# A decoder step on one core: another recorded order of the attention's blocks

## The chip, the cores and the metric

The kernel runs on one core of a Trainium2 chip. A core has TensorE (PE) for matmuls, VectorE (DVE), ScalarE (ACT) and GpSimd (POOL) for elementwise work, and SyncE (SP), which here only issues DMAs. Each engine takes its instructions in the order in which they were emitted. The metric is the device time of one execution in microseconds (us). The kernel before took 1256.64 us, the median of three runs (1256.27 to 1256.86).

## The reference, cut to what matters

One inference step of a two-layer trunk with D = 1024, for a prompt of 512 tokens and for 8 samples of 8 new tokens each. Layer 0 is a recurrent block with a SwiGLU; then keys and values are made once; layer 1 is attention over a sliding window of 128 with a learned sink per head, and a SwiGLU. The change lies in the attention:

```python
q = apply_partial_rope((h @ attn_w_q[j]).reshape(B, T, N_HEADS, HEAD_DIM), pos)
out = sliding_sink_attention(q, k_all, v_all, attn_sinks[j], p0) @ attn_w_o[j]
x = x + g1[:, None, :] * out

def sliding_sink_attention(q, k_all, v_all, sinks, p0):
    ...
    s = jnp.einsum('bnqkgd,bnskd->bnkgqs', qg, kb).astype(jnp.float32) * (HEAD_DIM ** -0.5)
    ...
    m = jnp.maximum(jnp.max(s, axis=-1, keepdims=True), sink)
    e = jnp.exp(s - m)
    p = e / (jnp.sum(e, axis=-1, keepdims=True) + jnp.exp(sink - m))
    o = jnp.einsum('bnkgqs,bnskd->bnqkgd', p.astype(vb.dtype), vb)
    return o.reshape(B, T, N_HEADS * HEAD_DIM)
```

A prompt block of 128 queries sees its own 128 keys and the 128 before them; the 8 tokens of a sample see the 128 cached keys of that sample and the new ones.

## The kernel before, in words

Activations lie transposed, features on the 128 partitions, tokens along the free dimension. The tokens are split into two halves, A and B (h = 0 and 1 in the code), each with 256 prompt tokens and 4 samples of 8 tokens: 288 columns. Weights are fp32 and are cut, after loading, into a high part and the rest (`convert`, line 1034: a cast on ScalarE and a subtraction on VectorE), and so are the activations; one product of a 128-column block of a 1024-row weight with one half is 8 x 3 = 24 matmuls of 128x288 (`product`, line 1070). The converted weights lie in ten slots named `wh`, two for each weight block; two of the ten hold the keys during attention. `load_more` (line 1025) issues the weight loads on SP's queue.

The attention stage is a list of blocks, written down by hand in the string `ATT` (line 53). A name is a letter, a number and the half:

- `q0` to `q7`: one of the eight blocks of the query projection, a product of 24 matmuls. Its evacuation (`rope`, line 1547) is a shuffle, a multiplication and an addition on VectorE and one multiplication and two small copies on GpSimd. `q7` also opens the half's operand buffer `h` for the output projection (`attn_open`, line 1805): the chunks that are finished by then are cut into two parts there.
- `a0` to `a7`: attention of the prompt for two heads of that query block (`attn_chunk`, line 1650). Scores (matmuls over 64 rows, `mm<-wh,sl` in the profile), maxima with the mask on VectorE (`CUSTOM_DVE_ANT_0`), exponentials on ScalarE, sums and reciprocals on VectorE, scaling on three engines. A second part follows later: transposes, copies, the value product (`ada<-td,sl`) and its cut into two parts.
- `s0` to `s3`: attention of one sample for all heads (`attn_sample`, line 1730): two DMAs for the cached keys and values, transposes of the keys, scores (`mm<-ta,reg`, `mm<-tb,reg`), softmax; a second part with transposes and value products (`mm<-td,reg`, `mm<-td,wh`). The cached keys and values of samples 0, 3 and 6 share one buffer, those of 1, 4 and 7 another, those of 2 and 5 a third (line 1737); s0B to s3B are samples 4 to 7.
- `f`: closes a half (`attn_fin`, line 1829): writes the new keys out and puts the samples' results into the operand buffer `h`, which every output product of that half reads.
- `o0` to `o2`: the first output products of a half (24 matmuls each). The rest of them, and the half B of these, follow in the next stage.

The second part of a block is not recorded at once. It waits in a list (`flush`, line 1638) until one or two more blocks have been recorded; `f` records all that wait. All `a` and `s` blocks take their small statistics (maximum, sum, reciprocal) from two tiles in turn (`new_stat`, line 1646).

The string does not set the order on the engines directly. Every operation is first recorded with its reads and writes; its place in the record is its priority. Then a planner (`schedule`, line 227) with costs written into the code goes through the record and emits, on each engine, the operation that can start first. Ties and near ties go by the record: the key is the possible start plus 0.75 ns for each place (lines 39 and 344). On TensorE an operation of another shape (scores over 64 rows, products with 64 columns) counts as 100 ns later than one of the same shape (line 339). It looks up to 600 places ahead of the oldest operation that is left (lines 50 and 316), and SP's DMAs stay within 60 places of their order. PSUM has six tiles for products, scores and transposes (line 43) and two for value products. What an engine runs on the chip is the planner's order.

Of the kernel before, what the change touches and what calls it, by code (L numbers as in the profile page):

```python
# [49 lines left out]
WIN = 600  # L50

RNN = "x0 x1 x2 g0 g1 x3 y0 y1 x4 g2 g3 x5 y2 x6 y3 g4 g5 x7 y4 y5 g6 g7 y7 y6"
ATT = "q0A q2A a0A q1A q0B a2A q1B q3A a0B q2B q4A a1A a1B a4A a3A q3B a2B q5A q4B a3B q6A a5A q5B q7A a6A a4B s0A q6B a5B s1A s2A s3A q7B a7A s0B fA s2B a6B a7B s1B o0A s3B o1A o2A fB"
LOOK = {"PE": 24, "DVE": 24, "ACT": 24, "POOL": 24, "SP": 24}
NRAW = 4
FILL = 250
# [459 lines left out]
def trunk_kernel(ctx, tc, a):  # L516
# [1339 lines left out]
    each = []  # L1856
    for w in ATT.split():
        h, n = "AB".index(w[-1]), int(w[1:-1] or 0)
# [245 lines left out]
```

## Time and profile before

| | |
|---|---|
| timed runs | 1256.27, 1256.64, 1256.86 us |
| profiled execution | 1259.39 us |
| its span, first to last instruction | 1257.6 us |
| TensorE busy | 1243.6 us (99%) |
| VectorE, ScalarE, GpSimd busy | 897.9, 659.4, 481.4 us |
| mean granted TensorE clock | 0.995 |
| attention stage, about | 700 to 809 us of the span |

The page of the profile gives each engine's busy time, the chain of work that ended last, and groups of instructions by the names of their tiles. All instructions stand under line 489, the line of the helper that records them, so they are told apart by tile names, shapes and times. A windows view gives, for stretches of time, the busy time of each engine with the number of its instructions, the granted clock of TensorE as a share of full speed, the share of DMA time and GB/s. A timeline row gives start, length, engine, operation and tiles, and the number of equal instructions that were merged.

### The profile page before, as it was taken

The numbers are of one execution on the slowest core, as the hardware profiler recorded it, in microseconds if no ns is written. First come the engines' busy times: TensorE is split into PE (matmuls) and PEld (weight loads), VectorE is DVE, ScalarE is ACT, GpSimd is POOL, SyncE is SP. The second block draws the span as 40 slices with busy tenths as digits, with TensorE's granted clock in tenths as the row PEclk, the third lists the DMA queues.
The fourth block names the chain that finished last, engine by engine and source line by source line (L and its number), as shares of the span: only waits on it lengthen the run. The fifth ranks groups of instructions, "written<-read, shape, count | busy, mean of one in ns | idle before, by whom it ended". The sixth has DMA issues, their size and how long they took to land.

```text
span 1257.6 us, 25624 instructions
## 1 busy us (share of the span) xinstructions
PE 1243.6 (99%) x9674; PEld 1181.1 (94%) x9674; DVE 897.9 (71%) x2192; ACT 659.4 (52%) x1474; POOL 481.4 (38%) x671
## 2 busy tenths in 40 slices
PE   8999999999999999999999999999999999999997
PEld 7888999999998999999999987999999999999997
DVE  6989784776674676467579878558767658756856
ACT  4798963753342354145357678538425425524533
POOL 3478550133451453345125446100435336435510
PEclk9999999999999999999999999999999999999999
DMA  9966454417455645445423322232333323323222
GB/s 313 300 203 222 155 166 154 156 56 214 152 178 179 202 128 181 156 153 184 116 77 73 78 60 60 77 99 97 91 95 85 101 84 100 96 76 100 79 91 76
DMA packets 221838, 165.42 MB, mean 132 GB/s; under 512 B 23725, under 2 KB 206985, under 8 KB 221682
## 3 DMA queue, kind: packets, MB, share of 16 engines
q1 hardware_dynamic: 221266, 163.45, 42.4%
q8 instruction: 76, 1.25, 0.4%
q14 instruction: 48, 0.39, 0.1%
q0 software_dynamic: 448, 0.32, 0.1%
HBM read 160.85 MB, written 4.87 MB: 132 GB/s over the span
## 4 chain that ended last, share of the span: by engine, by line
PE 90%; DVE 4%; ACT 4%; issue 1%; DMA 0%; POOL 0%; DVEq 0%; ACTq 0%; SPq 0%; POOLq 0%
PE mm L489 86%; PE ada L489 5%; ACT ta L489 1%; DVE sl L489 1%; ACT sl L489 1%; DVE wh L489 1%; DVE ta L489 1%; ACT tb L489 0%; DVE tb L489 0%; ACT wh L489 0%; ACT L489 0%; DMA raw<-in_ffn_w_out_dram 0%; DVE h L489 0%; ACT td L489 0%; ACT h L489 0%
## 5 line engine op out<-in xcount | busy, mean ns | idle before, releaser
L489 PE MATMUL mm<-h,wh 128*128 128x288 f32 x4128 | 590.5, 297 | 1.1 <-DVE wh L489 0.9
L489 PEld LDWEIGHTS mm<-h,wh 128*128 128x128 f32 x4128 | 559.3, 188 | 12.9 <-issue 6.0
L489 PE MATMUL mm<-sl,wh 128*128 128x288 f32 x3218 | 461.1, 296 | 0.6 <-DVE wh L489 0.5
L489 PEld LDWEIGHTS mm<-sl,wh 128*128 128x128 f32 x3218 | 436.7, 188 | 7.5 <-issue 5.9
L489 ACT CAST wh<-raw 128x512 fp32r<-128x512 f32 (+3 forms) x388 | 268.8, 711 | 300.6 <-PE mm L489 188.4
L489 DVE TENSOR_TENSOR wh<-raw,wh 128x512 fp32r<-128x512 f32 (+3 forms) x388 | 352.7, 929 | 50.0 <-ACT wh L489 45.0
L489 POOL TENSOR_TENSOR raw<-raw 128x512 f32<-128x512 f32 x76 | 112.2, 1476 | 191.4 <-DVE wh L489 135.0
L489 DVE SCALAR_TENSOR_TENSOR x<-mm,mods,x 128x256 f32<-128x256 f32 x160 | 77.2, 483 | 125.9 <-PE mm L489 125.4
L489 POOL TENSOR_TENSOR x<-x,ta 128x32 f32<-128x32 f32 x120 | 42.4, 353 | 243.9 <-DVE ta L489 243.8
L489 POOL TENSOR_TENSOR raw<-raw,raw 128x512 f32<-128x512 f32 x76 | 113.0, 1486 | 4.2
L489 PE MATMUL mm<-tb,wh 128*128 128x288 f32 (+1 forms) x488 | 89.0, 297 | 1.6 <-DVE td L489 1.6
L489 POOL TENSOR_TENSOR td<-td,td 128x288 f32<-128x288 f32 x38 | 31.1, 820 | 131.3 <-ACT td L489 131.3
L489 PEld LDWEIGHTS mm<-tb,wh 128*128 128x128 f32 x488 | 72.8, 188 | 3.0 <-DVE td L489 2.0
L489 ACT ACTIVATE ta<-x 128x288 f32<-128x288 f32 (+1 forms) x56 | 24.3, 442 | 62.5 <-POOL x L489 44.0
L489 PE MATMUL mm<-ta,wh 128*128 128x288 f32 (+1 forms) x254 | 56.0, 297 | 0.0
L489 DVE TENSOR_TENSOR td<-mm,td 128x288 f32<-128x288 f32 x76 | 33.6, 452 | 25.4 <-PE mm L489 25.1
L489 PE MATMUL ada<-reg,cz 128*32 128x512 f32 (+1 forms) x408 | 47.2, 547 | 0.0
L489 PEld LDWEIGHTS mm<-ta,wh 128*128 128x128 f32 x254 | 41.7, 188 | 1.7 <-ACT sl L489 0.8
L489 ACT COPY td<-mm 128x256 f32<-128x256 f32 (+1 forms) x102 | 33.6, 354 | 13.9 <-PE mm L489 13.6
L489 DVE TENSOR_TENSOR sl<-td,sl 128x288 fp32r<-128x288 f32 x50 | 33.7, 674 | 6.0 <-ACT sl L489 5.7
L489 ACT ACTIVATE ta<-ta,stat 128x256 f32<-128x256 f32 (+2 forms) x72 | 32.5, 474 | 9.4 <-DVE stat L489 9.1
L489 DVE TENSOR_TENSOR mm<-mm,ta 128x288 f32<-128x288 f32 x38 | 17.7, 465 | 27.5 <-PE mm L489 27.5
(213 smaller groups left out, 1305.3 us busy)
## 6 DMA issues: line engine op xcount, KB each, us to landing
raw<-in_ffn_w_in_dram SPq DMA_DIRECT2D x88, 512.0 KB
reg<-in_ada_w_dram SPq DMA_DIRECT2D x72, 512.0 KB
raw<-in_ffn_w_out_dram SPq DMA_DIRECT2D x32, 384.0 KB
raw<-in_ffn_w_out_dram SPq DMA_DIRECT2D x32, 320.0 KB
raw<-in_rnn_w_in_dram SPq DMA_DIRECT2D x16, 512.0 KB
reg<-in_kv_ada_w_dram SPq DMA_DIRECT2D x14, 512.0 KB
wh<-in_ada_w_dram SPq DMA_DIRECT2D x24, 256.0 KB
raw<-in_rnn_w_out_dram SPq DMA_DIRECT2D x8, 512.0 KB
```

The costliest lines, as they stand in the source:

```text
L489: self.rec.add(eng, lambda: getattr(obj, name)(*map(real, args), **{k: real(v) for k, v in kw.items()}), cost, outs, ins, func, lat, port, ...
```

## The change

One string is replaced. In words, for what moves:

- front: q0B and q1A are recorded ahead of q2A and a0A; a4A ahead of a1A and a1B; q3B ahead of a3A;
- the end of half A: q6B is recorded behind s3A, next to q7B, where it stood between s0A and a5B;
- behind a7A: s0B, s1B, a6B, fA, a7B, o0A, s2B, s3B where there was s0B, fA, s2B, a6B, a7B, s1B, o0A, s3B.

The stretch from q5A to s0A is the same. The set of blocks, and so of operations, is the same.

```diff
-ATT = "q0A q2A a0A q1A q0B a2A q1B q3A a0B q2B q4A a1A a1B a4A a3A q3B a2B q5A q4B a3B q6A a5A q5B q7A a6A a4B s0A q6B a5B s1A s2A s3A q7B a7A s0B fA s2B a6B a7B s1B o0A s3B o1A o2A fB"
+ATT = "q0A q0B q1A q2A a0A a2A q1B q3A a0B q2B q4A a4A a1A a1B q3B a3A a2B q5A q4B a3B q6A a5A q5B q7A a6A a4B s0A a5B s1A s2A s3A q6B q7B a7A s0B s1B a6B fA a7B o0A s2B s3B o1A o2A fB"
```

## The prediction, made before the change was run

> **What bounds the kernel now.** I read the page first, then the chain, then the windows of the attention stage (it runs from about 700 to 809 us), and last the rows of single engines inside it.
>
> ```profile
> span 1257.6 us, 25624 instructions
> ...
> PE 1243.6 (99%) x9674; PEld 1181.1 (94%) x9674; DVE 897.9 (71%) x2192; ACT 659.4 (52%) x1474; POOL 481.4 (38%) x671
> ...
> PE 90%; DVE 4%; ACT 4%; issue 1%; DMA 0%; POOL 0%; DVEq 0%; ACTq 0%; SPq 0%; POOLq 0%
> ```
>
> TensorE has work for 1243.6 of 1257.6 us and the chain that ends last lies on it for 90%. To find the rest I cut the attention stage into pieces of 10 us (columns: TensorE, its weight loads, VectorE, ScalarE, GpSimd busy; granted clock; DMA):
>
> ```profile
> 720.00:730.00 10.00, 10.00 (x93) 8.71 (x92) 8.49 (x43) 9.87 (x36) 3.06 (x6) 1.00 0.18 52
> 730.00:740.00 10.00, 10.00 (x95) 8.75 (x93) 8.22 (x34) 7.18 (x26) 4.34 (x10) 1.00 0.01 4
> 740.00:750.00 10.00, 10.00 (x86) 9.61 (x83) 8.73 (x41) 7.46 (x26) 3.74 (x7) 1.00 0.45 133
> ...
> 760.00:770.00 10.00, 10.00 (x91) 9.33 (x91) 9.22 (x38) 9.70 (x39) 4.76 (x13) 1.00 0.05 15
> 770.00:780.00 10.00, 9.54 (x94) 7.53 (x90) 8.78 (x38) 8.32 (x31) 8.76 (x17) 1.00 0.20 57
> 780.00:790.00 10.00, 9.87 (x60) 6.89 (x58) 6.25 (x36) 5.95 (x24) 1.98 (x9) 0.66 0.55 161
> 790.00:800.00 10.00, 10.00 (x89) 9.83 (x89) 4.59 (x21) 5.44 (x19) 2.07 (x5) 1.00 0.22 65
> ```
>
> Read the PE column and PEclk. TensorE is full until 770 and again from 790. Between, it has 0.59 us without work, and from 780 to 790 the granted clock is 0.66: 10 x (1 - 0.66) = 3.4 us of clock are lost. VectorE and ScalarE are nearly full from 760 to 770 (9.22 and 9.70). They, not TensorE, set the speed of the softmax there. The next view is the same stage for the weight products alone, matmuls that read the activations `h` (columns: busy time with their number, clock, DMA):
>
> ```profile
> 752.50:759.00 6.50, 0.11 (x1) 1.00 0.01 3
> 759.00:770.00 11.00, 7.58 (x48) 1.00 0.05 13
> 770.00:780.80 10.80, 0.00 (x0) 1.00 0.23 66
> 780.80:787.70 6.90, 0.00 (x0) 0.51 0.67 196
> 787.70:809.00 21.30, 14.84 (x90) 1.00 0.17 49
> ```
>
> The products of the query projection are used up before 770. From 770 to 787.7 there is not one of them. These 17.7 us hold only sample blocks, transposes and the last chunks, small matmuls whose inputs come from the softmax of the block before, and here the clock falls to 0.51 for 6.9 us. After 787.7 the output products run packed and TensorE stays full but for the last few microseconds of the kernel (350.23 of the last 357.60, below), so every microsecond by which they begin earlier or later goes into the end one for one. That start waits for two things: the value product of chunk a7A and the closing step fA of the first half.
>
> ```profile
> 900.00:1257.60 357.60, 350.23 (x2653) 349.15 (x2651) 243.59 (x504) 149.67 (x290) 132.00 (x135) 0.99 0.31 92
> ```
>
> I named the blocks by laying the recorded order beside the rows:
>
> ```profile
> 764.27 0.38 PE L489 MATMUL mm<-ident,wh 128*128 128x128 f32 x2
> ...
> 765.29 0.30 PE L489 MATMUL mm<-ta,reg 128*64 128x160 f32 x1
> ...
> 766.13 3.31 PE L489 MATMUL mm<-h,wh 128*128 128x288 f32 x23
> ...
> 770.65 0.30 PE L489 MATMUL mm<-ta,reg 128*64 128x160 f32 x1
> ...
> 787.75 0.65 PE L489 MATMUL mm<-h,wh 128*128 128x288 f32 x3
> ```
>
> The 23 matmuls at 766.13 are q7B, the last product. At 764.27 stand two transposes of sample block s2A, in the first cluster after q6B; at 765.29 the scores of s0A and s1A; at 770.65 the scores of s2A and s3A, only after q7B and a value product; at 787.75 the first output product, o0A.
>
> **The change part by part.** No instruction is added or dropped. Each engine gets the same set; priorities, the order of the two shared statistics tiles, and the positions in the queues change.
>
> *Statistics tiles.* Attention blocks use two tiles in turn, so a block's maxima wait for the block two places before it. Up to a7A the turn of the second stretch (a5A to a7A) stays the same, block by block. At the tail s1B takes the place of s2B and the reverse; the two are alike in size. In the front a4A takes the place of a1A, and a1A and a1B fall back by one.
>
> *q6B moved behind s3A* (24 matmuls; on VectorE a shuffle, a product and a sum; on GpSimd one product and two copies; no DMA). The first half's sample blocks now rank ahead of it. Its evacuation shares VectorE with the maxima of a5B, and behind these the chain is:
>
> ```profile
> 767.63 1.23 DVE L489 TENSOR_TENSOR wh<-raw,wh 128x1024 fp32r<-128x1024 f32 x1
> 768.77 0.41 DVE L489 TENSOR_TENSOR stat<-stat 128x4 f32<-128x4 f32 x1
> ...
> 771.50 0.31 DVE L489 CUSTOM_DVE_ANT_0 ta<-mm,reg 128x160 f32<-128x160 f32 x1
> ...
> 775.74 0.27 DVE L489 CUSTOM_DVE_ANT_0 ta<-mm,reg 128x128 f32<-128x128 f32 x1
> ```
>
> At 767.63 the low-part conversion of output weight 2 (1.23 us) runs ahead of the sum of a5B at 768.77, which holds the tile that s2A needs. That tile is free at 768.77 + 0.41 = 769.18, but s2A's maximum starts at 771.50, since its scores are issued at 770.65. That is 2.3 us on the chain a5B, s2A, a7A (775.74), a7A's value product, o0A. In the new order the transposes of s1A and s2A rank ahead of q6B's 24 matmuls, so s2A can be ready when the scores of s0A and s1A go at 765.29, and 769.18 becomes the bound. I take -2.3 us. The conversion needs the slots that q6 leaves (keys, q6, q7 and outputs 0 and 1 hold the ten), so it moves behind a later q6B. That is worth at most 768.77 - 767.63 = 1.1 us; as a5B's exponentials still end inside this time I take half, -0.5 us. Bounds of both: -3.4 if all of it counts; 0 if the planner fills the same gaps with q6B as now; above, +3.3 us, the length of one product (the row at 766.13), if one more product stands between s2A's transposes and its scores. What hides q6B itself today is the wait of the softmax chain from 759 to 770, where 7.58 us of products lie; if that cover is gone, q6B moves into the hole at 770 and fills it, which costs nothing.
>
> *q7B, a7A, s0B* keep their places; s3A, q6B and q7B now follow one another. q7B also carries six copies on ScalarE and six subtractions on GpSimd that open the second half; they stay ahead of a7A, as now: 0.
>
> *The tail.* s1B (two DMAs, four matmul steps, three ScalarE, four GpSimd and three VectorE steps, and behind them four matmul steps and two VectorE steps for its values) moves ahead of a6B; s2B moves behind o0A. What decides is the DMA queue, which issues in order:
>
> ```profile
> 759.45 0.33 SPq L489 DMA_DIRECT2D reg<-in_cache_k_dram  x1
> 771.98 0.33 SPq L489 DMA_DIRECT2D reg<-in_cache_v_dram  x1
> ```
>
> The second cache load of s3A held SP's queue from 759.45 to 771.98. s1B's key load goes to the tile that s2A leaves, behind that same wait; its value load needs s2A finished. s2B has an own tile that comes free with s3A. The scores of either wait for a statistics tile behind a7A anyway: 0, within 0.7 us either way (two loads of 0.33 us that change places). fA (two transposes, three ScalarE steps, one VectorE step, eight small output DMAs) is recorded behind s1B and a6B, and a6B's value steps ahead of it. Its inputs come from s3A, so it still becomes ready with it; its DMAs fall behind two more cache loads and nobody on the chip waits for them: 0. o0A is recorded one block earlier, and its four weight loads with it; they fill tiles needed after 800: 0.
>
> *The front.* q0B, q1A ahead of q2A and a0A: 48 matmuls of the same length in another order with TensorE full, and a0A's scores wait for nothing but a statistics tile: 0. a4A ahead of a1A, a1B, and q3B ahead of a3A:
>
> ```profile
> 714.44 0.28 DVE L489 CUSTOM_DVE_ANT_0 ta<-mm,reg 128x128 f32<-128x128 f32 x1
> ...
> 717.77 0.45 DVE L489 TENSOR_TENSOR sl<-mm,ta 128x288 f32<-128x288 f32 x1
> ```
>
> At 714.44 a1A's maxima begin. In the new order that turn belongs to a4A, whose queries are finished only at 717.77 + 0.45 = 718.2. So the softmax falls back by 3.8 us here. TensorE has q3B as cover (3.3 us of product) and stays full. The lag has to be made up before the products run out: from 730 to 740 ScalarE is busy 7.18 of 10 and VectorE 8.22 of 10, from 740 to 750 7.46 and 8.73. Together 5.4 us of ScalarE and 3.0 us of VectorE are free, against at most 3.8 us that slipped. I take 0, with +3.8 us as the upper end and 0 as the lower.
>
> *Changes of shape on TensorE.* Each switch between products and the 64-row or 64-column batches costs about a quarter of a microsecond (1.5 us in 6 cases, in the row below, for the value products from 745 to 810), and the new order makes a few more or fewer: 0, within 0.5 us either way.
>
> ```profile
> PEld ada L489 <- issue: 1.5, 6, 0.7
> ```
>
> **Sum.** -2.3 - 0.5 + 0 = -2.8 us. The profiled execution took 1259.39 us (span 1257.6, 1.8 around it), 2.75 us above the median of the timed runs, 1256.64. On the profiled one it gives 1256.6, on the median 1253.8 us. The clock loss is left in place: the stretch without products only gets shorter, from 17.7 to about 15 us.
>
> **The rivals.**
>
> *The clock keeps full speed (faster still).* The clock fell at 780.8 with TensorE busy 9.54 of 10 in the slice before. So it was not idle time as the rows count it, and the stretch without products is the one thing that sets the place apart. If a part of q6B or q7B falls into 770 to 787, the 6.9 x 0.49 = 3.4 us come back: 1253.8 - 3.4 = 1250.4. Against it: the planner issues whatever is ready first, and products always are. The Trainium skill ("TensorE: Matmul & The Clock Gate", part 1) says that the half clock comes after at least one idle window of about 3.4 us; by that rule alone no order of this kind matters, and nothing would be won here. This trace disagrees, as the rows above show no such idle time. Part 4 of the same page says that transposes do not count as busy in the same way, which would fit the stretch.
>
> *The planner undoes it (no change).* It takes on each engine the instruction that can start first and weighs the recorded position with 0.75 ns a place. q6B falls back by some 110 places, 80 ns. Today it runs in gaps of the softmax; if it runs in the same gaps, all of the second stretch stays as it is: 1256.6.
>
> *The lag of the front is not made up (slower).* If a7A's maxima, at 775.74 today, come the whole 3.8 us later, the start of o0A does too: 1256.6 + 3.8 = 1260.4. It decides against the forecast once more than 2.8 + 2.5 us of delay is left at a7A, or more than 2.5 us if the gain fails. For it: ScalarE had 9.87 of 10 from 720 to 730 and 9.70 from 760 to 770, so what slips there is not made up there. Against it: the free 5.4 and 3.0 us between.
>
> *The scores crowd out the products (slower).* Sample scores that are ready early hold a PSUM tile until their statistics tile is free, and there are six such tiles. If q7B has to wait for one, it ends behind the chain: + 3.3 us, 1259.9. It decides if TensorE shows more than 2.5 us without work between 755 and 770, where it has none now.
>
> **How the numbers follow.** A measurement of this kernel tells about 0.2% (2.5 us) from no change. Forecast 0.31, with an own range from 1252.7 (the whole -3.4 and -0.5 for shapes) to 1255.4 (half of the 2.3 us); clock kept 0.08; no change 0.29; lag 0.20; crowding 0.12. Faster takes the first two, less the 0.03 of the forecast that would end within 0.2%: 0.36. Within 0.2% is 0.29 + 0.03 = 0.32, slower 0.20 + 0.12 = 0.32. The lower end reaches a little into the case of the clock, 1250.8, and the upper end to the whole lag, 1260.6.
>
> **What would show it.** Right: s2A's maximum begins within half a microsecond of the end of a5B's sum, a7A's maxima come 2 to 3 us earlier against the start of the stage, and the first output product follows the last query product by about 15 us. The lag: a4A's maxima begin only after q4A's queries, and the blocks up to a5A run later than before. The clock: no slice under 0.9 near 780. Wrong altogether: q6B in the same gaps, or a hole for TensorE before 770.

## The result, and the profile after

| | before | after |
|---|---|---|
| median of 15 timed runs each, us | 1256.86 | 1259.91 |
| ratio, 95% interval | | 1.002 (1.0013 to 1.0027) |
| profiled execution, us | 1259.39 | 1259.54 |
| its span, us | 1257.6 | 1257.8 |
| mean granted clock | 0.995 | 0.998 |

The change costs about 3 us, 0.2%. The forecast was 1253.8 us, 2.8 us faster. The two profiled executions look alike only because that of before has a stretch of half clock: a second trace of the same kernel (experiment 4) took 1256.63 us and has none. Of the 15 timed runs of before four lie between 1258.5 and 1259.1 us, and of 102 more, taken beside the experiments, 22 lie above 1258 us at a lower mean clock (0.994 to 0.997). The same stretch of time, the windows view of the first trace of before and then of the second (columns as in the prediction):

```profile
780.84:787.66 6.82, 6.69 (x36) 4.06 (x33) 3.77 (x23) 3.06 (x13) 1.23 (x4) 0.50 0.67 196
```

```profile
780.84:787.66 6.82, 6.39 (x56) 5.20 (x56) 6.01 (x39) 5.27 (x23) 0.93 (x3) 1.00 0.67 198
```

Clock 0.50 in the one, 1.00 in the other, with one and the same order. From here on, "before" is the second trace. The page of after:

```profile
span 1257.8 us, 25623 instructions
...
PE 1242.1 (99%) x9674; PEld 1180.4 (94%) x9674; DVE 897.1 (71%) x2192; ACT 658.6 (52%) x1474; POOL 480.7 (38%) x671
...
PE 89%; DVE 5%; ACT 4%; issue 1%; DMA 1%; POOL 0%; DVEq 0%; ACTq 0%; SPq 0%; POOLq 0%
```

TensorE is still busy for 99%; in the chain of waits a DMA now has 1% where it had 0%. The attention stage by windows, before and then after:

```profile
700.00:710.00 10.00, 10.00 (x81) 9.61 (x81) 9.30 (x42) 7.39 (x24) 4.84 (x10) 1.00 0.36 90
710.00:720.00 10.00, 10.00 (x94) 8.28 (x93) 8.60 (x48) 7.60 (x30) 4.38 (x13) 1.00 0.19 54
760.00:770.00 10.00, 10.00 (x96) 9.41 (x97) 9.22 (x38) 9.70 (x38) 5.32 (x14) 1.00 0.04 13
770.00:780.00 10.00, 9.54 (x87) 7.29 (x83) 8.51 (x39) 8.13 (x30) 8.77 (x20) 1.00 0.22 63
780.00:790.00 10.00, 9.57 (x81) 7.88 (x80) 7.81 (x46) 8.05 (x33) 2.36 (x8) 1.00 0.66 192
```

```profile
700.00:710.00 10.00, 9.01 (x71) 8.23 (x70) 7.33 (x38) 4.25 (x16) 3.65 (x7) 1.00 0.19 53
710.00:720.00 10.00, 9.89 (x91) 8.60 (x93) 7.85 (x36) 7.95 (x28) 4.88 (x13) 1.00 0.19 54
...
760.00:770.00 10.00, 9.65 (x90) 8.40 (x88) 8.05 (x41) 9.31 (x39) 2.76 (x10) 1.00 0.05 14
770.00:780.00 10.00, 9.88 (x99) 8.33 (x95) 9.14 (x40) 8.02 (x26) 7.73 (x18) 1.00 0.19 54
780.00:790.00 10.00, 9.96 (x79) 7.78 (x79) 8.94 (x49) 9.04 (x39) 5.39 (x13) 1.00 0.26 70
```

TensorE loses 0.99 us at 700 to 710, in the front, where the prediction had nothing; from 770 to 790 it has less idle time than before (0.16 us against 0.89), and from 760 to 770 more (0.35 us against none).

To place the loss I compare the start of the same instruction in both traces: the first shuffle of q0A on VectorE, which opens the stage, and a weight conversion behind its last block. Before, then after:

```profile
687.42 0.49 DVE L489 STREAM_SHUFFLE ta<-mm 128x288 f32<-128x288 f32 x1
814.69 1.23 DVE L489 TENSOR_TENSOR wh<-raw,wh 128x1024 fp32r<-128x1024 f32 x1 [0.36 <-ACT wh L489]
```

```profile
687.92 0.50 DVE L489 STREAM_SHUFFLE ta<-mm 128x288 f32<-128x288 f32 x1
816.65 1.23 DVE L489 TENSOR_TENSOR wh<-raw,wh 128x1024 fp32r<-128x1024 f32 x1 [0.37 <-ACT wh L489]
```

The stage takes 127.27 us before and 128.73 after: 1.46 us are lost inside it. The 0.50 us at its opening arise before any instruction has changed its place: over all the traces this opening lies between 686.70 and 688.51 and has nothing to do with the order. Behind the stage more is lost, at one weight load of the feed-forward stage. Its second weight comes in loads of 320 KB, and ScalarE casts each when it has landed. The casts of loads 2 to 5 (columns: start, length, engine, operation, tiles, shapes; in brackets the idle time ahead and who ended it), before, then after:

```profile
900.92 0.73 ACT L489 CAST wh<-raw 128x640 fp32r<-128x640 f32 x1 [2.21 <-DMA raw<-in_ffn_w_out_dram]
904.62 0.73 ACT L489 CAST wh<-raw 128x640 fp32r<-128x640 f32 x1 [0.90 <-DMA raw<-in_ffn_w_out_dram]
906.06 0.73 ACT L489 CAST wh<-raw 128x640 fp32r<-128x640 f32 x1
909.39 0.73 ACT L489 CAST wh<-raw 128x640 fp32r<-128x640 f32 x1 [2.60 <-PE mm L489]
```

```profile
902.57 0.73 ACT L489 CAST wh<-raw 128x640 fp32r<-128x640 f32 x1 [1.96 <-DMA raw<-in_ffn_w_out_dram]
907.09 0.72 ACT L489 CAST wh<-raw 128x640 fp32r<-128x640 f32 x1 [1.49 <-DMA raw<-in_ffn_w_out_dram]
908.34 0.73 ACT L489 CAST wh<-raw 128x640 fp32r<-128x640 f32 x1
911.86 0.73 ACT L489 CAST wh<-raw 128x640 fp32r<-128x640 f32 x1 [2.79 <-PE mm L489]
```

From cast 2 to cast 3 pass 3.70 us before and 4.52 after, from cast 2 to cast 5 8.47 and 9.29. TensorE itself waits there for 0.48 us, which it does not before:

```profile
908.50 1.71 PE L489 MATMUL mm<-h,wh 128*128 128x288 f32 x11 [0.48 <-ACT td L489]
```

So the lateness against before is 0.50 us at 687, 1.96 at 816, 2.47 at 911 and 2.9 at the end (span 1254.9 against 1257.8).

### The profile page after: what moved, and what is told of

The parts are those of the page before. It is cut to its first block, busy times and chain, and to the rows that moved or that the text cites. A ratio compares the mean times of both kernels' runs of the same rounds, so it can differ in the third digit from the quotient of the medians.

```text
span 1257.8 us, 25623 instructions
## 1 busy us (share of the span) xinstructions
PE 1242.1 (99%) x9674; PEld 1180.4 (94%) x9674; DVE 897.1 (71%) x2192; ACT 658.6 (52%) x1474; POOL 480.7 (38%) x671
## 4 chain that ended last, share of the span: by engine, by line
PE 89%; DVE 5%; ACT 4%; issue 1%; DMA 1%; POOL 0%; DVEq 0%; ACTq 0%; SPq 0%; POOLq 0%
PE mm L489 84%; PE ada L489 5%; ACT ta L489 1%; DVE ta L489 1%; DVE sl L489 1%; DMA raw<-in_ffn_w_out_dram 1%; ACT sl L489 1%; ACT tb L489 1%; DVE tb L489 1%; DVE wh L489 1%; ACT L489 1%; ACT td L489 0%; ACT wh L489 0%; DVE td L489 0%; DVE h L489 0%
```

## The experiments

The theories:

- 1: the new front makes the softmax late and TensorE waits (1a: because of q0B and q1A; 1b: because of a4A).
- 2: q6B and q7B together push a7A back.
- 3: the weight load is late by chance.
- 4: TensorE's own work, and not the softmax, fills the stretch before a7A.
- 5: the order makes the load late.
- 6: a fetch of instructions makes it late.

The table has all runs, with the number of the experiment. The stage is the time between the two rows above (shuffle of q0A and weight conversion); a row without a ratio is a single execution; the last two columns are the casts' distances.

| run | median us | before, beside it | ratio (95%) | stage us | cast 2 to 3 | cast 2 to 5 |
|---|---|---|---|---|---|---|
| before, again (4) | 1256.63 | 1257.11 | | 127.27 | 3.70 | 8.47 |
| changed kernel | 1259.91 | 1256.86 | 1.002 (1.0013 to 1.0027) | 128.73 | 4.52 | 9.29 |
| front alone (1) | 1259.29 | 1257.11 | 1.0011 (1.0002 to 1.0021) | 128.83 | 3.48 | 8.39 |
| middle alone (2) | 1257.66 | 1257.11 | 1.0005 (0.9996 to 1.0013) | 127.22 | 4.32 | 9.10 |
| tail alone (3) | 1257.48 | 1257.11 | 1.0002 (0.9993 to 1.0011) | 127.36 | 3.42 | 8.33 |
| q0B, q1A early (5) | 1258.79 | 1256.81 | 1.0007 (0.9996 to 1.0017) | 128.55 | 3.60 | 8.52 |
| a4A early (6) | 1257.14 | 1256.81 | 1.0004 (0.9995 to 1.0012) | 127.04 | 3.47 | 8.39 |
| middle and tail (7) | 1258.27 | 1256.81 | 1.0008 (1.0 to 1.0017) | 127.20 | 4.60 | 9.37 |
| before, q6B short (8) | 1259.03 | 1256.81 | 1.0019 (1.001 to 1.0028) | 129.41 | 3.48 | 8.38 |
| changed, again (9) | 1259.89 | 1256.75 | 1.0024 (1.0015 to 1.0033) | 128.76 | 4.47 | 9.24 |
| middle, again (10) | 1257.16 | 1256.75 | | 127.20 | 4.38 | 9.15 |
| front and tail (11) | 1259.18 | 1256.75 | 1.0016 (1.0007 to 1.0025) | 128.91 | 3.93 | 8.71 |
| changed, fetch moved (12) | 1258.92 | 1256.98 | 1.0011 (1.0002 to 1.002) | 128.74 | 3.59 | 8.50 |
| before, fetch moved (13) | 1256.8 | 1256.98 | 0.9999 (0.999 to 1.0008) | 127.17 | 3.48 | 8.39 |

A ratio is estimated from all the runs and is not the quotient of the two medians: for q0B and q1A early the medians differ by 1.98 us, the ratio says 0.9 us, and its interval contains no change at all. The intervals are about 1 us wide to either side. Parts of 1 us are therefore judged by the traces, where the stage repeats to 0.1 us for one and the same order at full clock (127.27 and 127.17; 128.73, 128.76 and 128.74; 127.22 and 127.20).

**1. The front alone.** Only the front of the new string:

```diff
-q0A q2A a0A q1A q0B a2A q1B q3A a0B q2B q4A a1A a1B a4A a3A q3B a2B
+q0A q0B q1A q2A a0A a2A q1B q3A a0B q2B q4A a4A a1A a1B q3B a3A a2B
```

> Only the front of the order is the new one (q0B and q1A early, a4A ahead of a1A and a1B, q3B ahead of a3A); the rest is as before. Theory 1, the lag of the front stays: in the trace of the changed kernel the blocks from a2B to a6A stand 1.5 us later than before, although TensorE is full. If that is the cause, this run alone is 1.2 to 1.8 us slower than before (1258 to 1258.5 us against 1256.6) and shows the same 1.5 us from 743 us on. Theory 2, the two products in a row behind s3A: no effect here, within 0.5 us of before. Theory 3, the late weight load at 907 us: this run shows it or not whatever its front is.

The stage takes 128.83 us, 1.56 more than before, as theory 1 says; the load at 907 us is not late (cast 2 to 3: 3.48). The front carries the whole loss of the stage.

**2. The middle alone.**

```diff
-s0A q6B a5B s1A s2A s3A q7B a7A s0B
+s0A a5B s1A s2A s3A q6B q7B a7A s0B
```

> Only q6B is moved behind s3A, next to q7B; front and tail are as before. The prediction's step: 2.3 to 2.8 us faster (1253.8 to 1254.3 us). Theory 1 (the front is the cause of the loss): 0 to 1.3 us faster, since s2A's maxima gained 1.3 us against the blocks before them. Theory 2: q6B and q7B now stand as 48 matmuls ahead of a7A's value product and push the start of o0A back; 1 to 3 us slower, a7A's maxima 2 to 3 us later (at 778 us instead of 775.74).

The stage takes 127.22 us, 0.05 less than before: neither the prediction's gain nor a loss. On VectorE, the maxima of s2A and of a7A, before, then in this run:

```profile
770.96 0.31 DVE L489 CUSTOM_DVE_ANT_0 ta<-mm,reg 128x160 f32<-128x160 f32 x1
...
775.20 0.27 DVE L489 CUSTOM_DVE_ANT_0 ta<-mm,reg 128x128 f32<-128x128 f32 x1
```

```profile
768.93 0.30 DVE L489 CUSTOM_DVE_ANT_0 ta<-mm,reg 128x160 f32<-128x160 f32 x1
...
775.42 0.28 DVE L489 CUSTOM_DVE_ANT_0 ta<-mm,reg 128x128 f32<-128x128 f32 x1
```

The stage opens at 686.70 here, 0.72 us earlier than before. Against its opening s2A gains 770.96 - 768.93 - 0.72 = 1.3 us, and a7A loses 775.42 - 775.20 + 0.72 = 0.9 us. What stands between them is most of a product. The scores of s2A, the product next to them and the scores of a7A on TensorE, before, then here:

```profile
765.57 3.31 PE L489 MATMUL mm<-h,wh 128*128 128x288 f32 x23
...
770.11 0.30 PE L489 MATMUL mm<-ta,reg 128*64 128x160 f32 x1
...
774.14 1.79 PE L489 MATMUL mm<-wh,sl 64*128 64x128 f32 x16
```

```profile
767.90 0.30 PE L489 MATMUL mm<-ta,reg 128*64 128x160 f32 x1
...
770.56 2.38 PE L489 MATMUL mm<-h,wh 128*128 128x288 f32 x16
...
774.11 0.93 PE L489 MATMUL mm<-wh,sl 64*128 64x128 f32 x8
```

Before, q7B (23 of its 24 matmuls are in the row at 765.57) lies ahead of s2A's scores. Here 16 of its matmuls, 2.38 us, lie between the scores of s2A and those of a7A: 770.11 to 774.14 is 4.0 us, 767.90 to 774.11 is 6.2. What s2A won, a7A paid, and 0.9 us more. Theory 2 has the mechanism right and its price wrong: the first output product starts 0.6 us later against the opening (784.30 - 686.70 here, 784.44 - 687.42 before), and at the end of the stage nothing is left of it.

**3. The tail alone.**

```diff
-s0B fA s2B a6B a7B s1B o0A s3B o1A o2A fB
+s0B s1B a6B fA a7B o0A s2B s3B o1A o2A fB
```

> Only the blocks behind a7A stand in the new order (s1B and a6B ahead of fA, o0A ahead of s2B). Theories 1 and 2: within 0.7 us of before. If the loss lies here: 1 to 3 us slower, and the blocks between o0A and fB are late by that much, while all up to a7A stands at the places of before.

127.36 us, 0.1 more than before, although s1B and s2B change places by 11 to 15 us. The tail costs nothing.

**4. The kernel before, again.** No edit.

> The kernel before, once more, for a second trace of it. The clock theory: the half clock from 780.8 to 787.7 us in the first trace belongs to some executions alone; the 15 timed runs of before lie in two groups, about 1256.6 us (11 runs) and 1258.9 us (4 runs), and the profiled one, 1259.39, is of the second. If this one takes about 1256.6 us, its trace shows no half clock there, and the stage after 790 us stands 2 to 3 us earlier. Theory 3: if the wait for the weight load at 907 us is absent here and present in the changed kernel's repeats, it belongs to the change; if it comes and goes, it is chance.

1256.63 us and no half clock. Of the 2.75 us by which the first trace stood above the median, 2.3 belong to the half clock (its stage takes 129.61 us) and 0.6 to a later opening (688.00); 0.2 come back behind the stage.

**5 and 6. The front in two parts.** First q0B and q1A alone:

```diff
-q0A q2A a0A q1A q0B a2A q1B
+q0A q0B q1A q2A a0A a2A q1B
```

> Of the new front only this: q0B and q1A ahead of q2A and a0A. The prediction had 0 for it. Theory 1a: in the changed kernel the scores of a0A start at 703.78 us (before: 700.02), fewer products are left between them and a0A's transposes, and TensorE then waits 1.10 us for a0A's exponentials. This run should show that wait of about 1.1 us at 709 to 711 us and be 1.2 to 1.6 us slower than before. Theory 1b (the prediction's reason: a4A in the turn of a1A): nothing here, within 0.3 us, and no such wait.

Then a4A and q3B alone:

```diff
-q4A a1A a1B a4A a3A q3B a2B
+q4A a4A a1A a1B q3B a3A a2B
```

> Of the new front only this: a4A ahead of a1A and a1B, q3B ahead of a3A. Theory 1a: within 0.4 us of before, although a1A and a1B come 4 to 8 us later, since TensorE has products of the queries as cover. Theory 1b: 1.2 to 1.6 us slower, the blocks from a2B on late by that much.

The first has a stage of 128.55 us, 1.28 more; the second one of 127.04, 0.2 less. Theory 1a holds by the traces, 1b falls. The cause can be read off TensorE's rows. Before: the scores of a0A, the products behind them, the first transposition of a0A's exponentials.

```profile
700.02 1.58 PE L489 MATMUL mm<-wh,sl 64*128 64x128 f32 x16
701.53 6.54 PE L489 MATMUL mm<-h,wh 128*128 128x288 f32 x47
707.90 0.27 PE L489 MATMUL mm<-ident,ta 128*128 128x128 f32 x1
```

With q0B and q1A early, and in the changed kernel:

```profile
703.62 1.58 PE L489 MATMUL mm<-wh,sl 64*128 64x128 f32 x16
705.13 3.73 PE L489 MATMUL mm<-h,wh 128*128 128x288 f32 x26
709.96 0.33 PE L489 MATMUL mm<-ident,ta 128*128 128x128 f32 x1 [1.10 <-ACT ta L489]
```

```profile
703.78 1.58 PE L489 MATMUL mm<-wh,sl 64*128 64x128 f32 x16
705.29 3.73 PE L489 MATMUL mm<-h,wh 128*128 128x288 f32 x26
710.11 0.33 PE L489 MATMUL mm<-ident,ta 128*128 128x128 f32 x1 [1.10 <-ACT ta L489]
```

The softmax of a0A needs 710.11 - 703.78 = 6.3 us from the first score to the first transposition. Before, 47 matmuls of products lie in between and the transposes come after 7.9 us; TensorE never waits. In the new front the scores come 3.8 us later (0.5 of them from the later opening), and the planner has put only 26 matmuls between, 3.73 us instead of 6.54. TensorE then waits 1.10 us for the exponentials, and as it is full afterwards the wait stays to the end. It is most of the 1.28 us; the rest was not followed up. The two parts alone give 1.28 - 0.23 = 1.05 us, the whole front 1.56. Most of the difference is a second wait, which only the five traces with the whole new front have, of 0.32 us ahead of 737.09 in the changed kernel, again for exponentials.

**7. Middle and tail without the front.** The changed string with the front of before.

```diff
-q0A q0B q1A q2A a0A a2A q1B q3A a0B q2B q4A a4A a1A a1B q3B a3A a2B
+q0A q2A a0A q1A q0B a2A q1B q3A a0B q2B q4A a1A a1B a4A a3A q3B a2B
```

> The changed kernel with the front of before: new middle and new tail together. If the parts add up (front +1.5 us, middle 0, tail 0 in the traces): within 0.5 us of before, about 1256.6 us, and 2 to 3 us faster than the changed kernel in the timed runs (1259.9). If the loss needs all three parts together: 1 us or more slower than before.

In the stage the parts add up: 127.20 us, 0.07 less than before. But the run is 1.46 us above before by its median. By its trace the loss arises behind the stage: cast 2 to cast 5 takes 9.37 us, and TensorE waits 0.71 us there. So there is a second, separate loss, which needs no new front; run 2 has it as well (0.47 us).

**8. Less of q6B.** In the product of q6B, the two low-part terms are left out.

```diff
             hi, lo = u.block(k)
+            if cut[0]:
+                T.matmul(o, hi, xh, start=(first and k == 0), stop=(last and k == n - 1))
+                continue
```

> The kernel before, with 16 of the 24 matmuls of product q6B left out (the two low-part terms), so q6B is not computed fully; everything else is issued. 16 matmuls take 16 x 3.31/23 = 2.3 us. The prediction's view (from 759 to 770 us the products only fill the wait of the softmax, and a chain over a5B, s2A and a7A sets the start of o0A): 0, within 0.5 us, and TensorE stands idle about 2 us more between 690 and 810 us. Theory 4 (TensorE's own work fills the stretch, and the softmax chain has slack): about 2 us faster, with no more idle time than before (0.96 us from 690 to 810).

It came out otherwise than both theories expected: the stage is 2.1 us longer, with 2.3 us less work. From 690 to 810 us TensorE, before, then here:

```profile
690.00:810.00 120.00, 119.04 (x1033) 105.94 (x1032) 92.81 (x407) 83.70 (x294) 51.95 (x111) 1.00 0.27 73
```

```profile
690.00:810.00 120.00, 116.67 (x1001) 101.83 (x1000) 92.53 (x406) 83.59 (x293) 49.47 (x110) 1.00 0.26 69
```

TensorE is idle for 3.33 us instead of 0.96. With less to do TensorE only waits more, which speaks against theory 4. But the planner also laid the blocks in another order (a sample's maxima stand at 762.06 us, where before the first are at 765.37), so the run does not measure the chain over s2A by itself. It decides neither view.

**9 to 11. Is the late load chance?** The changed kernel and the middle alone once more, without an edit, and the changed kernel with q6B back at its old place:

```diff
-s0A a5B s1A s2A s3A q6B q7B a7A
+s0A q6B a5B s1A s2A s3A q7B a7A
```

> The changed kernel once more, for a second trace. In its first trace, and in those of the two other runs with the new middle, the third load of the second FFN weight lets its cast start 4.3 to 4.6 us after the cast of the second one; in the seven traces with the old middle (before twice, front alone, tail alone, both parts of the front, the one with a shortened q6B) it is 3.4 to 3.7 us. Theory 5 (this late load belongs to the order): again 4.3 to 4.6 us here, the blocks behind 910 us late by 0.5 to 0.8 us more than those at 890. Chance: 3.4 to 3.7 us as likely as not.

> The run with only the new middle once more, one look. Theory 5: the third cast 4.3 to 4.6 us after the second, as in its first trace (4.32). Chance: 3.4 to 3.7 us.

> The changed kernel with q6B back at its place between s0A and a5B: new front and new tail, old middle. Theory 5 together with theory 1a: the stage of attention loses 1.3 to 1.7 us against before, as in the changed kernel, but the third cast comes 3.4 to 3.7 us after the second, and the kernel is 0.7 to 1 us faster than the changed one, 1.5 to 2.2 us slower than before. If the late load is chance or belongs to the new front: as slow as the changed kernel.

Cast 3 follows cast 2 after 4.47 and 4.38 us in the repeats and after 3.93 with the old middle. In all five traces with the new middle up to here it is 4.32 to 4.60, in the seven with the old middle ahead of run 11 3.42 to 3.70, and 3.93 in run 11. TensorE's own wait at the load (0.46 to 0.71 us) stands in those five traces and in no other. So it is not chance. Run 11 lies nearer to the old middle than to the new, but above the expected 3.4 to 3.7, and is 1.6 us longer in the stage as expected.

The trace has the landing of each of the load's sixteen parts, counted from its issue (901.82 us after, 899.93 before). After, fifteen have landed by 3.05 us and the last lands at 5.19; before, fifteen by 3.16 and the last at 4.61. One part of sixteen is late. In the same microseconds one packet of 16 KB goes over the queue that carries instructions: after, it begins 2.0 us after the issue of the load and ends at 3.65; before, it begins at 0.96 and ends at 2.74. In run 8, where it begins only at 4.1, the last part lands at 3.32, together with the others. From here comes theory 6. All fifteen traces agree with it: in the twelve in which the packet begins 0.8 to 2.2 us after the issue, the last part lands 1.5 to 2.1 us behind the packet's end (packet's end 1.84 to 2.74 us with the old middle, 3.27 to 3.81 with the new, 3.29 in run 11; last part at 3.88 to 4.61, 5.13 to 5.43, and 4.78); in runs 8, 12 and 13, in which it begins at 4.1 us or later, all sixteen have landed by 3.32. Why the packet ends later with the new middle was not tested.

**12 and 13. The fetch moved.** The kernel holds transpositions that only fill TensorE (the identity into a scratch tile, which nobody reads). In run 12, 32 of them are left out of the changed kernel; in run 13, 8 are left out of the kernel before:

```diff
+        fills = 0
         for op in order_:
+            if op.idle:
+                fills += 1
+                if 60 < fills <= 92:
+                    continue
             op.emit()
```

(In run 13 the bounds are 60 < fills <= 68.)

> The changed kernel, with 32 of the filling transpositions on TensorE left out (the identity transposed into a scratch tile, between about 19 and 31 us of the span, whose result nobody reads), so that every later fetch of TensorE's instructions comes 32 matmuls later, some 4.5 us at 0.14 us each. Theory 6: the third load of the second FFN weight is late because one of its sixteen parts lies behind a 16 KB fetch of instructions on the same DMA engine; in the changed kernel the fetch begins 2.0 us after that load is issued and ends 3.65 us after it, in the traces of the old middle it ends 1.8 to 2.7 us after it. Here the fetch falls behind the load: the third cast comes 3.3 to 3.6 us after the second (changed kernel: 4.52 and 4.47), and the blocks behind 912 us stand 0.6 to 0.9 us better against those at 895. The whole time: 0 to 0.9 us faster than the changed kernel, as other loads meet other fetches. If the fetch isn't the cause: 4.4 to 4.6 us as before.

> The kernel before, with 8 of the same filling transpositions left out, so that the fetch comes about 1.1 us later, where it is in the changed kernel. Theory 6: the third cast now comes 4.3 to 4.6 us after the second (before: 3.49 and 3.70) and the kernel loses 0.6 to 0.9 us behind 905 us, although its order is that of before. If the new order itself delays the load in another way: 3.4 to 3.7 us, no loss.

The instruction packet, in the view of the DMA queues (packets, MB, share of 16 engines): first the changed kernel, window 903 to 906 us; then run 12, where it is not in that window but in the one from 907 to 910.

```profile
q8 instruction: 1, 0.02, 3.4%
```

```profile
q8 instruction: 1, 0.02, 3.1%
```

And the casts of run 12:

```profile
902.59 0.73 ACT L489 CAST wh<-raw 128x640 fp32r<-128x640 f32 x1 [1.97 <-DMA raw<-in_ffn_w_out_dram]
906.18 0.73 ACT L489 CAST wh<-raw 128x640 fp32r<-128x640 f32 x1 [0.59 <-PE mm L489]
...
911.09 0.73 ACT L489 CAST wh<-raw 128x640 fp32r<-128x640 f32 x1 [2.40 <-PE mm L489]
```

3.59 us instead of 4.52, and what ends the wait is no longer the DMA; TensorE's wait at the load is gone too. The order is that of the changed kernel in everything that has a result; the stage takes 128.74 us as without the edit, and the median, 1258.92, is 1.94 us above before's, where the changed kernel stood 3.05 and 3.14 above. By the timed runs alone this gain is not clear, as the intervals overlap. Theory 6 holds in this direction by the trace. The edit did one thing more: with the fills gone TensorE runs at half clock from 22.60 to 29.43 us, and the mean clock is 0.995 in all eleven runs. The stage opens at 687.86 us all the same, as in the changed kernel (687.92 and 688.26), so this does not explain the gain. Run 13 missed its aim: the fetch moved by 3.5 us instead of 1.1, past the load (it begins 4.46 us after the issue), and nothing was lost. So that the load can also be delayed by moving the fetch onto it in the old order was not shown.

No new order beats before: the a4A part of the front gains 0.2 us in the stage, which its timed runs (1.0004) do not confirm.

## Why the prediction was wrong

**The base.** "The clock loss is left in place": it was there in the profiled execution, and not in the median one. I noted that the profiled execution stood 2.75 us above the median and that 3.4 us of clock were lost in it, and did not put the two together. The clock rival (1250.4) counted as a gain what most runs of before already had. Of the stretch without products I said that it "sets the place apart"; the second trace has the same order and clock 1.00, so the stretch alone does not bring the clock down. Nor are the about 15 us from the last query product to the first output product a sign of the gain: the second trace of before has 15.2 (768.88 + 0.38 to 784.44). Neither of the two rules of the Trainium skill that I weighed there ("TensorE: Matmul & The Clock Gate") is decided by these runs. The 6.83 us at half clock cost 2.3 us in the stage, not 3.4; why less was not tested.

**q6B moved behind s3A: -2.3 us.** The step that failed. s2A's maxima came 1.3 us earlier, not 2.3 (after the change they start at 771.71, 1.9 us behind the end of a5B's sum, where I wanted half a microsecond). And the gain did not go on to a7A: "q7B, a7A, s0B keep their places" held in the record only. On TensorE 16 of q7B's 24 matmuls slid from ahead of s2A's scores to behind them, and a7A's maxima came 0.9 us later instead of 2 to 3 earlier. I had seen that the stretch has 0.59 us without work and that products are its filling, but moved one of them as if the chain beside it were free of TensorE. This term measured 0 (the middle alone: stage 127.22 us against 127.27). So for this term the rival of no change had the right time, but not the cause: q6B did move.

**The conversion: -0.5 us.** It moved away as foretold (from 767.09 to 775.11); with the chain not gaining, it is worth nothing.

**The tail: 0 within 0.7.** Right, 0.1 us.

**The front.** "q0B, q1A ahead of q2A and a0A: 0" is the second step that failed, and the dearer one: +1.28 us alone, 1.56 with the rest of the new front. I asked whether a0A's scores had to wait, and not what TensorE would still have to do while a0A's softmax ran. The a4A term, where I saw the danger and put the upper end of 3.8 us, is right at 0: a1A and a1B do fall back by 4 to 8 us, the products of the queries cover it. So the rival of the lag (1260.4) came near to the measured time with another cause, and less than half of its lag. The rival of the crowded scores has the measured time almost exactly, 1259.9, and that is luck: it wanted more than 2.5 us without work on TensorE between 755 and 770 us, and there are 0.35. Most of q7B did fall behind s2A's scores, but in the stage that cost nothing.

**Not in the prediction at all:** the late load, 0.8 us from cast 2 to cast 5 and 0.48 us of waiting on TensorE, and about 0.4 us between 912 us and the end that no run explains. With 1.46 in the stage and 0.5 net at the load these are 2.4 us in the traces; the medians have 3.05. The changes of shape, 0 in the sum, were not measured by themselves.

## What to carry to other kernels

Ahead of a change of order, count what the engine that never idles will still have to do behind each score until its softmax is through: here 6.3 us must be covered, and products that are moved forward are missing as cover later. If a block is moved off a chain of waits beside a full engine, its work comes up again at a later place on that engine: look which step of the chain then stands behind it. And if the profiled execution lies above the median, look for what in it explains the difference before any of it is used as a term of a sum.

## What the runs showed of the hardware

A fetch of instructions can delay a load of data: with a 16 KB packet of 1.6 us on the instruction queue (0.9 to 2.4 in the other traces) one of the sixteen parts of a 320 KB load landed at 5.19 us, where the other fifteen had landed by 3.05; with the packet moved behind the load all sixteen landed by 3.14. That the packet and the late part share one DMA engine is inferred, as the trace names no engine. A program that differs only ahead of the place can so lose 0.5 to 0.7 us on TensorE at a load that nobody touched. The Trainium skill ("Runtime: NRT & Kernel Launch", section on instruction fetch mechanics) says that instructions come in blocks of 16 KiB over the sequencer's own queue and that the cost is mostly hidden. The size agrees with the packets of 16384 bytes here; the cost was not hidden where a weight load was due at the same time, as run 12 shows.

The half clock of 6.83 us came in one of two traces of the same program, with TensorE busy for 9.54 of 10 us in the window ahead in both. What decides it there stays open. In run 12, where filling work was left out, a half clock of the same length (6.83 us) came with TensorE busy for only 7.76 us of the 10 from 10 to 20 us; the changed kernel, with the fills, has 8.58 there and keeps clock 1.00.
